# Moving the high part of the MLP input's last kt by 224 bytes, and its low part's product ahead of it

## The chip, the cores and the metric

The kernel runs on one core of a Trainium2 chip. The metric is the device time of one execution in microseconds (us). Three runs of the kernel before took 2049.33, 2052.9 and 2054.07 us; the median is 2052.9. One execution was also profiled, and each statement about single instructions comes from that trace. Engines are named as the profile names them: PE is TensorE's matmuls, PEld its weight loads, DVE is VectorE, ACT is ScalarE, POOL is GpSimd, SP is SyncE.

## The reference

A two-layer encoder trunk over 256 tokens of width 2048, in float32. Each layer has attention (neighbourhood attention in the first, grouped-query attention in the second, each beside four cross-attention heads into 256 memory tokens) and then a dense MLP. The part that the change touches is the MLP's first product:

```python
n = rms_norm(h, mlp_norm[i])
h = h + jnp.square(jax.nn.relu(n @ w_up[i])) @ w_down[i]
```

Here n is 256 x 2048, w_up 2048 x 8192 and w_down 8192 x 2048.

## The kernel before, in words

**Split operands.** Each float32 operand of a large product is held as two parts, high and low, both of the type fp32r: the high part is a rounded copy that ACT writes, the low part is the rest, which DVE computes. A product is then three matmuls that add into the same PSUM tile: high by high, high weights by low input, low weights by high input.

**The MLP's input.** `hT` is the normed input of the MLP, transposed, features on the 128 partitions: 16 kt of 128 features, and for each kt 512 elements along a partition, 256 tokens of the high part and then 256 of the low part. It lies in a tile of the tag "wide", made by `wide` (L434), which has 128 elements (512 bytes) of room beyond the 16 x 512 that it uses. `wide` takes an offset in bytes; `hT` uses 0, the attention input `nT` uses 480. `o_done` (L620) makes `hT` once in each layer (L628) and fills it kt by kt: `transposed` (L323) has PE transpose into PSUM, and `split_pair` (L335) has ACT write the high part and DVE the low part. After the last kt, DVE adds to `h` (L661).

**The up-projection.** A chunk of w_up is 128 columns wide, 64 chunks in each layer, 128 in all. For each chunk `u_products` (L707) runs over the 16 kt with three matmuls each, 48 in all, each with the weights stationary (128 x 128) and 256 tokens of `hT` moving: L713 is the high weights by the high input, L714 the high weights by the low input, L715 the low weights by the high input. The weights come as two halves of 8 kt, split by `half_of_side` (L717) into the tiles uh and ul.

**The down-projection and the order.** The 64 chunks are eight parts of eight. `add_mlp` (L948) plans part 0 of the up-projection alone, eight chunks in a row. From then on each chunk of part p + 1 goes together with one step of the down-projection of part p, 56 steps in each layer, 112 in all. Such a step is a sum of seven products in the manner of Strassen. `down_grains` (L785) makes it in two groups, FIRST with three products on the tiles bh and bl (nine matmuls), and SECOND with four on th and tl (twelve); here the activations a_s are stationary and 512 columns of weights move (L828 to L830). A scheduler orders the instructions of each engine; on PE it makes mostly the cycle: the 48 matmuls of a chunk, the 12 of SECOND, the 9 of FIRST, the next chunk. The weights' last part of eight goes through plain products (L217 to L221).

**Where tiles start.** Some tiles are placed at chosen offsets along the partition. `MOVING_AT` = 160 bytes is added to uh and ul where they are the moving operand of a plain product and not the stationary one of the up-projection.

The functions that the change touches, and what calls them:

Of the kernel before, what the change touches and what calls it, by code (L numbers as in the profile page):

```python
# [11 lines left out]
F32R = mybir.dt.float32r  # L12
# [5 lines left out]
P = 128  # L18
D = 2048
SEQ = 256  # L20
NT = SEQ // P
KT = D // P
# [18 lines left out]
GUARD = 3  # L41

MOVING_AT = 160
MASKED = -1e30


# [10 lines left out]
class Work:  # L57


    def __init__(self, kind, src, acts, first, begins, last, start, done):  # L60
        self.kind, self.src, self.acts = kind, src, acts
        self.first, self.begins, self.last, self.start, self.done = first, begins, last, start, done
        self.early = False


class Grain:
# [7 lines left out]
def encoder_kernel(ctx: ExitStack, tc: tile.TileContext, t: dict, out: bass.AP):  # L74
    nc = tc.nc
# [3 lines left out]
    def opened(name, side="left", space=None, bufs=1):  # L79
        kw = {"space": space} if space else {}  # L80
        manager = tc.tile_pool(name=name, bufs=bufs, side=side, reuse_waits="tile", **kw)
        pools[name] = manager, manager.__enter__()
        return pools[name][1]

    def closed(*names):
        for name in names:
            pools.pop(name)[0].__exit__(None, None, None)

    const = opened("const")
    keep = opened("keep")  # L90
# [28 lines left out]
    for j in range(8):  # L119
        s = slice(j * 512, (j + 1) * 512)  # L120
        nc.sync.dma_start(mem0[:, s], t["memT"][:, s])
        if j % 2 == 0:
            s = slice(j * 256, (j + 2) * 256)
# [25 lines left out]
    def halves_of(w):  # L149
# [6 lines left out]
        def prep_early(hf):  # L156
            tiles[hf] = half_of_side(tiles["raw"], hf, MOVING_AT)

# [39 lines left out]
    def later(n, fn, *args):  # L198
        pending.append((state["tick"] + n, fn, args))
# [124 lines left out]
    def transposed(dst, src, ks, which):  # L324

        for a in range(0, len(ks), 2):
            pt = at.att.tile([P, 2, SEQ], F32, tag="att", name="pt_n")
            for b, k in enumerate(ks[a : a + 2]):
                for i in range(NT):
                    nc.tensor.transpose(pt[:, b, i * P : (i + 1) * P], src(i, k), ident)  # L330
            for b, k in enumerate(ks[a : a + 2]):
                last = split_pair(dst, pt[:, b, :], which, k)
        return last
# [100 lines left out]
    def wide(name, at=0):  # L434
        room = keep.tile([P, KT * 512 + P], F32R, tag="wide", name=name)
        return room[:, at // 4 : at // 4 + KT * 512].rearrange("p (a b) -> p a b", b=512)

    def keys(name):
        return at.work.tile([P, NMH, 512], F32R, tag="keys", bufs=1, name=name)

# [160 lines left out]
    def sum_squares(which, i, nb):  # L601
        sq = at.side.tile([P, 512], BF16, tag="junk", bufs=1, name="sq")
        nc.scalar.activation(sq, h[:, i, nb * 512 : (nb + 1) * 512], AF.Square,
                             accum_out=ssq[which][:, i, nb : nb + 1])

    def mean_square(which, n, name):

        s = small.tile([P, NT], F32, tag="ss0", name="ss_t")
        nc.vector.tensor_reduce(s, ssq[which][:, :, :n], axis=AX.X, op=ALU.add)
        v = keep.tile([P, NT], F32, tag=name, name=name)  # L610
        nc.vector.tensor_scalar(v, s, 1.0 / (n * 512), EPS, op0=ALU.mult, op1=ALU.add)
        return v
# [7 lines left out]
    def o_done(layer, nb):  # L620
        which = 2 * layer

        def guard():

            box["near"] = mean_square(which, GUARD, "near")
            box["scale"] = keep.tile([P, NT], F32, tag="scale", name="scale")
            nc.gpsimd.tensor_tensor(box["scale"], box["near"], mhalf[:, :NT], op=ALU.pow)
            box["hT"] = wide(f"hT{layer}")  # L628

        def begun():  # L630

            y = at.side.tile([P, NT, 512], F32, tag="T", bufs=2, name="h_s")
            for i in range(NT):
                nc.scalar.activation(y[:, i, :], h[:, i, D - 512 :], AF.Copy, scale=box["scale"][:, i : i + 1])
            box["begun"] = y

        def scaled(b):
            y = at.side.tile([P, NT, 512], F32, tag="T", bufs=2, name="h_s")
            for i in range(NT):
                nc.scalar.activation(y[:, i, :], h[:, i, b * 512 : (b + 1) * 512], AF.Copy,  # L640
                                     scale=box["scale"][:, i : i + 1])
            transposed(box["hT"], lambda i, k: y[:, i, k % 4 * P : (k % 4 + 1) * P],
                       list(range(b * 4, b * 4 + 4)), (G_M0, G_M1)[layer])

        def inv():

            v = mean_square(which, 4, "full")
            box["inv"] = keep.tile([P, NT], F32, tag="inv", name="inv")
            nc.vector.reciprocal(v, v)
            nc.vector.tensor_tensor(box["inv"], v, box["near"], op=ALU.mult)  # L650
            box["ninv"] = keep.tile([P, NT], F32, tag="ninv", name="ninv")
            nc.vector.tensor_scalar(box["ninv"], box["inv"], -1.0, None, op0=ALU.mult)

        def f(w):
            if nb == 0:
                closed("work")
                at.side = opened("side", side="right")
            def add():
                for i in range(NT):
                    hs = h[:, i, nb * 512 : (nb + 1) * 512]  # L660
                    nc.vector.tensor_tensor(hs, w.ps[i], hs, op=ALU.add)  # L661

            def squares():
                for i in range(NT):
                    sum_squares(which, i, nb)

            if nb < 3:
                add()
                squares()
            if nb == GUARD - 1:  # L670
                later(1, guard)
                for b in range(GUARD):
                    later(2 + 2 * b, scaled, b)
                later(7, begun)
            if nb == 3:
                y = box["begun"]
                for i in range(NT):
                    nc.vector.scalar_tensor_tensor(y[:, i, :], w.ps[i], box["scale"][:, i : i + 1], y[:, i, :],
                                                   op0=ALU.mult, op1=ALU.add)
                box["ready"] = transposed(box["hT"], lambda i, k: y[:, i, k % 4 * P : (k % 4 + 1) * P],  # L680
                                          list(range(12, KT)), (G_M0, G_M1)[layer])
                later(8, past, add)
                later(10, past, squares)
                later(12, past, inv)
        return f
# [21 lines left out]
    def u_products(ps, k0, nk, hi, lo):  # L707

        acts = box["hT"]
        for j in range(nk):  # L710
            k = k0 + j
            s = slice(j * P, (j + 1) * P)
            nc.tensor.matmul(ps, hi[:, s], acts[:, k, :SEQ], start=k == 0, stop=False)  # L713
            nc.tensor.matmul(ps, hi[:, s], acts[:, k, SEQ:], start=False, stop=False)  # L714
            nc.tensor.matmul(ps, lo[:, s], acts[:, k, :SEQ], start=False, stop=k == KT - 1)  # L715

    def half_of_side(raw, hf, place=0):  # L717
        s = slice(place // 4, place // 4 + HALF)
        tiles = tuple(at.side.tile([P, HALF + 64], F32R, tag=n, bufs=2, name=n)[:, s] for n in ("uh", "ul"))
        box.setdefault("splits", []).append(split(*tiles, raw[:, hf * HALF : (hf + 1) * HALF]))  # L720
        return tiles
# [6 lines left out]
    def up_grains(layer, part, m):  # L728
# [8 lines left out]
        def run(hf):  # L737
            if hf == 0:
                if part == 0:
                    own["ps"] = at.acc.tile([P, 512], F32, tag="acc", name="ps_u")[:, :SEQ]  # L740
                else:
                    if part == 1 and m == 0:
                        closed("ps_att", "ps_acc")
                        at.sums = opened("ps_sums", space=bass.MemoryType.PSUM)
                        box["ps"] = {}
                        box["unused"] = set()
                    own["ps"] = at.sums.tile([P, 512], F32, tag="up", name="ps_u")[:, :SEQ]
            u_products(own["ps"], hf * (KT // 2), KT // 2, *own.pop(hf))
# [144 lines left out]
    def plain_grains(layer, nb):  # L893
# [9 lines left out]
        def prep(c, hf):  # L903
            if c == 0:
                own[c, hf] = half_of_side(own[0], hf, MOVING_AT)
            else:
# [275 lines left out]
def expanded_bias(rpb):  # L1182
# [6 lines left out]
    dc = np.clip(cols[None, :] - cols[:, None] + WIN_W - 1, 0, 2 * WIN_W - 2)  # L1189
    res = np.full((nh, 2, GRID_W, BJ, GRID_W), MASKED, np.float32)  # L1190
    for r in range(2):
        for j in range(BJ):
            dr = j + ROWS + 1 - r
            res[:, r, :, j, :] = np.where(inside[None], rpb[:, dr][:, dc], np.float32(MASKED))
    return res.reshape(nh, P, BJ * GRID_W)
# [64 lines left out]
```

## Time and profile before

| What | Value |
|---|---|
| Median of three runs | 2052.9 us |
| Profiled execution | 2051.05 us |
| Its span, first to last instruction | 2049.3 us |
| PE busy | 2029.9 us (99%) |
| Mean granted TensorE clock | 0.999 |
| Up-projection matmuls (L713, L714, L715) | 3 x 2048, of 128 x 256 |
| Down-projection matmuls on th and tl | 3 x 448, of 128 x 512 |
| Down-projection matmuls on bh and bl | 3 x 336, of 128 x 512 |

A row of a group in the profile gives the line, the engine, the operation, the tiles (written <- read), the shape, the count, then the busy time in us and the mean duration of one in ns, and last the idle time of the engine just before them with what ended it. Matmuls are pipelined: the next starts before the last has ended, and the ends are modelled. So the time from one start to the next says how fast PE goes, and the durations of one shape differ by as much as these steps do. A row of the timeline gives the start and the duration in us, the engine, the line, the operation and the tiles.

### The profile page before, as it was taken

How to read it: one execution, taken by the hardware profiler on the slowest of the kernel's cores; microseconds unless marked ns; L12 is line 12 of the kernel's file. 1: busy time of each engine (PE TensorE's matmuls, PEld its weight loads, DVE VectorE, ACT ScalarE, POOL GpSimd, SP SyncE). 2: the span in 40 equal slices, each digit the busy share in tenths (PEclk: the TensorE clock that was granted, in tenths of full speed). 3: DMA queues.
4: the chain of work that ended last, by engine and by line, in shares of the span. 5: the costliest groups of instructions: out<-in, count | busy, mean ns of one | idle time of the engine just before them, and what ended most of it. 6: DMA issues, size and time to landing. Idle time of an engine off the chain costs nothing.

```text
span 2049.3 us, 31582 instructions
## 1 busy us (share of the span) xinstructions
PE 2029.9 (99%) x12516; PEld 1813.1 (88%) x12516; DVE 1669.0 (81%) x2061; ACT 1252.6 (61%) x1652; POOL 119.3 (6%) x144
## 2 busy tenths in 40 slices
PE   8999999999999999999999999999999999999998
PEld 7888888889999999999988888889999999999996
DVE  6767666558999999999897667657989999999896
ACT  6755555556666666666656557556666666666664
POOL 0000000000000000000000001000000000000000
PEclk9999999999999999999999999999999999999999
DMA  7755554727777787787765554537877777777773
GB/s 280 283 190 179 190 176 169 276 86 228 230 231 231 218 242 226 222 245 220 231 219 200 180 184 144 187 122 222 246 228 228 224 230 228 231 230 226 232 222 132
DMA packets 93429, 433.79 MB, mean 212 GB/s; under 512 B 10464, under 2 KB 12128, under 8 KB 60128
## 3 DMA queue, kind: packets, MB, share of 16 engines
q1 hardware_dynamic: 75456, 398.47, 57.7%
q0 software_dynamic: 16816, 31.46, 8.7%
q8 instruction: 98, 1.61, 0.3%
q10 hardware_dynamic: 1008, 1.84, 0.3%
q14 instruction: 51, 0.42, 0.1%
HBM read 398.17 MB, written 4.19 MB: 196 GB/s over the span
## 4 chain that ended last, share of the span: by engine, by line
PE 98%; DVE 0%; ACT 0%; issue 0%; DMA 0%; POOLq 0%; POOL 0%; SPq 0%; ACTq 0%
PE ps_u L715 11%; PE ps_u L713 11%; PE ps_u L714 11%; PE p L828 9%; PE p L829 9%; PE p L830 9%; PE ps_m L217 8%; PE ps_m L220 8%; PE ps_m L221 8%; PE ps_s L230 7%; PE ps_s L233 3%; PE pt_a L393 1%; PE pt_n L330 1%; PE av L401 0%; PE sc_ps L367 0%
## 5 line engine op out<-in xcount | busy, mean ns | idle before, releaser
L715 PE MATMUL ps_u<-hT,ul 128*128 128x256 f32 x2048 | 568.4, 278 | 1.8 <-DVE ul L313 1.8
L713 PE MATMUL ps_u<-hT,uh 128*128 128x256 f32 x2048 | 568.6, 278 | 0.1
L714 PE MATMUL ps_u<-hT,uh 128*128 128x256 f32 x2048 | 568.0, 277 | 0.0
L312 ACT ACTIVATE uh<-raw_U 128x1024 fp32r<-128x1024 f32 x278 | 294.9, 1062 | 320.0 <-PE ps_u L714 302.1
L313 DVE TENSOR_TENSOR lo<-raw,hi 128x1024 fp32r<-128x1024 f32 (+1 forms) x220 | 261.4, 1194 | 164.6 <-ACT hi L312 162.1
L713 PEld LDWEIGHTS ps_u<-hT,uh 128*128 128x128 f32 x2048 | 384.9, 188 | 5.7 <-ACT uh L312 0.5
L715 PEld LDWEIGHTS ps_u<-hT,ul 128*128 128x128 f32 x2048 | 386.0, 189 | 3.6 <-DVE ul L313 2.6
L714 PEld LDWEIGHTS ps_u<-hT,uh 128*128 128x128 f32 x2048 | 384.4, 188 | 4.6
L313 DVE TENSOR_TENSOR ul<-raw_U,uh 128x1024 fp32r<-128x1024 f32 x278 | 337.6, 1219 | 40.0 <-ACT uh L312 39.8
L312 ACT ACTIVATE hi<-raw 128x1024 fp32r<-128x1024 f32 (+1 forms) x220 | 227.5, 1039 | 210.2 <-PE ps_m L221 119.0
L313 DVE TENSOR_TENSOR tl<-t,th 128x2048 fp32r<-128x2048 f32 x112 | 256.3, 2288 | 42.0 <-ACT th L312 41.8
L312 ACT ACTIVATE th<-t 128x2048 fp32r<-128x2048 f32 x112 | 215.1, 1921 | 123.2 <-PE p L830 118.6
L313 DVE TENSOR_TENSOR bl<-b,bh 128x1536 fp32r<-128x1536 f32 x112 | 196.1, 1751 | 0.3 <-ACT bh L312 0.2
L829 PE MATMUL p<-tl,a_s 128*128 128x512 f32 x448 | 177.2, 395 | 0.0
L830 PE MATMUL p<-th,a_s 128*128 128x512 f32 x448 | 174.4, 389 | 0.0
L312 ACT ACTIVATE bh<-b 128x1536 fp32r<-128x1536 f32 x112 | 166.2, 1484 | 7.4 <-PE p L830 1.3
L828 PE MATMUL p<-th,a_s 128*128 128x512 f32 x448 | 166.1, 395 | 0.0
L808 POOL DMA_DIRECT2D t<-b x112 | 97.1, 867 | 1160.8 <-ACT c L769 406.5
L230 PE MATMUL ps_s<-nT,hi 128*128 128x512 f32 x448 | 142.5, 397 | 0.0
L830 PE MATMUL p<-bh,a_s 128*128 128x512 f32 x336 | 131.1, 390 | 0.0
L829 PE MATMUL p<-bl,a_s 128*128 128x512 f32 x336 | 130.9, 390 | 0.0
L807 DVE TENSOR_TENSOR t<-t,b 128x512 f32<-128x512 f32 x112 | 77.1, 689 | 39.9 <-DMA t<-in_w_pair 35.0
(239 smaller groups left out, 3519.2 us busy)
## 6 DMA issues: line engine op xcount, KB each, us to landing
raw_U<-in_w_up SPq DMA_DIRECT2D x128, 1024.0 KB, 6.5
b<-in_w_pair SPq DMA_DIRECT2D x112, 768.0 KB, 4.6
raw<-in_w_o SPq DMA_DIRECT2D x32, 1024.0 KB, 4.9
t<-in_w_pair SPq DMA_DIRECT2D x112, 256.0 KB, 3.4
t<-b POOLq DMA_DIRECT2D x112, 256.0 KB, 6.8
raw<-in_w_b SPq DMA_DIRECT2D x21, 1024.0 KB, 5.0
raw<-in_w_av SPq DMA_DIRECT2D x12, 1024.0 KB, 4.9
raw<-in_w_aq SPq DMA_DIRECT2D x12, 1024.0 KB, 4.9
```

What stands on the lines that cost most here:

```text
L217: first = nc.tensor.matmul(w.ps[i], ah, hi[:, s], start=st, stop=False)
L220: nc.tensor.matmul(w.ps[i], ah, lo[:, s], start=False, stop=False)
L221: nc.tensor.matmul(w.ps[i], al, hi[:, s], start=False, stop=sp)
L230: nc.tensor.matmul(ps, hi[:, s], acts[:, k0 + j, :], start=k0 + j == 0, stop=False)
L312: first = nc.scalar.activation(dst_hi, src, AF.Copy)
L313: return first, nc.vector.tensor_tensor(dst_lo, src, dst_hi.bitcast(F32), op=ALU.subtract)
L713: nc.tensor.matmul(ps, hi[:, s], acts[:, k, :SEQ], start=k == 0, stop=False)
L714: nc.tensor.matmul(ps, hi[:, s], acts[:, k, SEQ:], start=False, stop=False)
L715: nc.tensor.matmul(ps, lo[:, s], acts[:, k, :SEQ], start=False, stop=k == KT - 1)
L828: nc.tensor.matmul(ps, a[:, 0, ai, :], hi[:, s], start=begins, stop=False)
L829: nc.tensor.matmul(ps, a[:, 0, ai, :], lo[:, s], start=False, stop=False)
L830: nc.tensor.matmul(ps, a[:, 1, ai, :], hi[:, s], start=False, stop=ends)
```

## The change

`hT` is now addressed through a small class. For the first 15 kt it gives the addresses of before. For the last kt the low part stands where the high one stood, and the high part 256 elements and 224 bytes (`LAST_AT`) further, in the room that the tile had beyond its 16 x 512 elements. In `u_products`, the last kt multiplies the high weights by the low part first and by the high part second. The third product is the same as before. The number and the shapes of all instructions stay.

```diff
+LAST_AT = 224
...
+class Shifted:
+    def __init__(self, room):
+        self.room = room
+
+    def __getitem__(self, key):
+        _, k, s = key
+        at = k * 512 + (s.start or 0)
+        if k == KT - 1:
+            at = k * 512 + (0 if s.start else SEQ + LAST_AT // 4)
+        return self.room[:, at : at + SEQ]
...
+    def shifted(name):
+        return Shifted(keep.tile([P, KT * 512 + P], F32R, tag="wide", name=name))
...
-            box["hT"] = wide(f"hT{layer}")
+            box["hT"] = shifted(f"hT{layer}")
...
-            nc.tensor.matmul(ps, hi[:, s], acts[:, k, :SEQ], start=k == 0, stop=False)
-            nc.tensor.matmul(ps, hi[:, s], acts[:, k, SEQ:], start=False, stop=False)
+            parts = (slice(0, SEQ), slice(SEQ, 512))
+            for n, x in enumerate(parts if k < KT - 1 else parts[::-1]):
+                nc.tensor.matmul(ps, hi[:, s], acts[:, k, x], start=k == n == 0, stop=False)
             nc.tensor.matmul(ps, lo[:, s], acts[:, k, :SEQ], start=False, stop=k == KT - 1)
```

## The prediction

> **What bounds the kernel now.** I read the page's first lines, then the chain of work that ended last, then the groups of the lines that the change touches and of the lines that follow them.
>
> ```profile
> span 2049.3 us, 31582 instructions
> PE 2029.9 (99%) x12516; PEld 1813.1 (88%) x12516; DVE 1669.0 (81%) x2061; ACT 1252.6 (61%) x1652; POOL 119.3 (6%) x144
> PE 98%; DVE 0%; ACT 0%; issue 0%; DMA 0%; POOLq 0%; POOL 0%; SPq 0%; ACTq 0%
> L715 PE MATMUL ps_u<-hT,ul 128*128 128x256 f32 x2048 | 568.4, 278 | 1.8 <-DVE ul L313 1.8
> L713 PE MATMUL ps_u<-hT,uh 128*128 128x256 f32 x2048 | 568.6, 278 | 0.1
> L714 PE MATMUL ps_u<-hT,uh 128*128 128x256 f32 x2048 | 568.0, 277 | 0.0
> L829 PE MATMUL p<-tl,a_s 128*128 128x512 f32 x448 | 177.2, 395 | 0.0
> L830 PE MATMUL p<-th,a_s 128*128 128x512 f32 x448 | 174.4, 389 | 0.0
> L828 PE MATMUL p<-th,a_s 128*128 128x512 f32 x448 | 166.1, 395 | 0.0
> L829 PE MATMUL p<-bl,a_s 128*128 128x512 f32 x336 | 130.9, 390 | 0.0
> ```
>
> TensorE carries 98% of the chain, and the idle time before the three up-projection lines is 1.9 us in all. No other engine can give time back, so the change counts only as far as matmuls start closer together or further apart. The numbers of matmuls stay: each of the 128 chunks of w_up takes 48 (16 kt of three). What can move is the step from one start to the next.
>
> The mean duration shows that step, because starts overlap: a duration is about 163 ns above the step to the next start. So I go by differences of durations within one width, and by starts in the timeline. One regular cycle of the MLP (a chunk of w_up, the 12 matmuls of SECOND on th and tl, the 9 of FIRST on bh and bl) looks like this, by groups in four windows: the first five matmuls of a chunk with the one before them, the middle of that chunk, its end with SECOND and FIRST, and a chunk of layer 0's part 0, where chunk follows on chunk.
>
> ```profile
> L713 PE MATMUL ps_u<-hT,uh 128*128 128x256 f32 x2 | 0.6, 284 | 0.0
> L714 PE MATMUL ps_u<-hT,uh 128*128 128x256 f32 x2 | 0.6, 282 | 0.0
> ...
> L713 PE MATMUL ps_u<-hT,uh 128*128 128x256 f32 x13 | 3.6, 276 | 0.0
> ...
> L829 PE MATMUL p<-tl,a_s 128*128 128x512 f32 x4 | 1.6, 397 | 0.0
> L828 PE MATMUL p<-th,a_s 128*128 128x512 f32 x4 | 1.6, 396 | 0.0
> L830 PE MATMUL p<-th,a_s 128*128 128x512 f32 x4 | 1.6, 389 | 0.0
> ...
> L829 PE MATMUL p<-bl,a_s 128*128 128x512 f32 x3 | 1.2, 389 | 0.0
> L715 PE MATMUL ps_u<-hT,ul 128*128 128x256 f32 x1 | 0.3, 280 | 0.0
> ...
> L714 PE MATMUL ps_u<-hT,uh 128*128 128x256 f32 x17 | 4.8, 281 | 0.0
> ```
>
> So one and the same matmul of 256 columns takes 276 ns at its best and 280 to 284 in three places: at the start of a chunk, as its last one, and all through some chunks. One of 512 columns takes 389 at its best and 396 or 397 just behind a chunk. The starts at one end of a chunk say the same:
>
> ```profile
> 548.51 0.28 PE L715 MATMUL ps_u<-hT,ul 128*128 128x256 f32 x1
> 548.63 0.40 PE L828 MATMUL p<-th,a_s 128*128 128x512 f32 x1
> ...
> 551.18 0.39 PE L830 MATMUL p<-th,a_s 128*128 128x512 f32 x1
> 551.41 0.39 PE L828 MATMUL p<-bh,a_s 128*128 128x512 f32 x1
> ...
> 553.45 0.28 PE L713 MATMUL ps_u<-hT,uh 128*128 128x256 f32 x1
> ```
>
> The nine of FIRST take 2.04 us, 227 ns each. The twelve of SECOND take 2.78 us where twelve times 227 is 2.72: **about 60 ns are lost behind each chunk**, and 4 more in its last matmul. Nothing waits there, the idle column is 0.0; these are slow steps. What changes at these places is the start address of the moving operand. In the built program hT's parts start 160 bytes past a multiple of 256, all 32 alike; th, tl, bh and bl start 128 past one. The stationary operands change too: uh and ul at 224 past, the activations a at 128. Inside a chunk nothing changes, and there the step is short.
>
> **The change part by part.** Order and waits first. On every engine the instructions are the same, in the same order; only the two matmuls of uh in the last kt change places, 128 times. ACT and DVE write the two parts of that kt in the order of before, so the first matmul on it in each layer now waits for DVE's part and not for ACT's. I cost that at nothing: DVE, in order, goes on to the add of L661 at 449.06 us, and the first matmul of the last kt is the fourth below, 1.85 us later. Had the cover gone, the price were one step, about 0.11 us, twice.
>
> ```profile
> 449.06 1.28 DVE L661 TENSOR_TENSOR h<-ps_m,h 128x512 f32<-128x512 f32 x2
> ...
> 450.91 0.28 PE L713 MATMUL ps_u<-hT,uh 128*128 128x256 f32 x1
> ```
>
> Addresses next. The low part now starts where the high one was, 160 past; the high part starts 1024 + 224 bytes further, which is 128 past a multiple of 256, as th does. The last three matmuls of a chunk read at 160, 128, 128, and the hand-over to th is at equal phase. The jump sits two matmuls earlier.
>
> What can be saved: the 60 ns behind a chunk and the 4 of its last matmul. Over the run, against 389 ns, the rows of th and tl give 448 x 6 + 448 x 6 + 448 x 0 ns = 5.4 us; 112 last matmuls by 4 ns are 0.4 us more. 5.8 us is the ceiling.
>
> What of it stays is not shown by any row directly, so I bound it by other places where matmuls of 256 columns hand over to matmuls of 512 whose moving operand starts at 128. Three such places, eleven steps each:
>
> ```profile
> 277.93 0.39 PE L220 MATMUL ps_m<-lo,nT 128*128 128x512 f32 x1
> ...
> 280.46 0.39 PE L217 MATMUL ps_m<-hi,nT 128*128 128x512 f32 x1
> ```
> ```profile
> 384.38 0.39 PE L220 MATMUL ps_m<-lo,cat 128*128 128x512 f32 x1
> ...
> 386.87 0.39 PE L217 MATMUL ps_m<-hi,cat 128*128 128x512 f32 x1
> ```
> ```profile
> 273.52 0.40 PE L217 MATMUL ps_m<-hi,nT 128*128 128x512 f32 x1
> ...
> 276.04 0.39 PE L221 MATMUL ps_m<-hi,nT 128*128 128x512 f32 x1
> ```
>
> Eleven steps at 226.7 ns are 2.49 us; these take 2.53, 2.49 and 2.52, so 37, 0 and 27 ns are lost. Behind a chunk of w_up the same count (548.63 to 551.18) is 2.55, which is 57. Undisturbed chunks thus give the worst entry I find. The first two places come from attention matmuls that start at 224, the third from matmuls that start at 128. I take the mean of the three, 21 ns, and keep 0 and 60 as ends.
>
> What is added: the last three matmuls of a chunk now stand at the jump. By the rows of a chunk's start a matmul near a jump takes 6 to 8 ns more than 276; I take 6 for each of three, 18, of which 4 were paid before: 14 more (ends: 8 and 20).
>
> The sum: 60 - 21 - 14 = 25 ns for each regular chunk. In 14 of the 112 chunks, seven in each layer, FIRST falls in after the chunk's second matmul, as here:
>
> ```profile
> 706.71 0.28 PE L714 MATMUL ps_u<-hT,uh 128*128 128x256 f32 x1
> 706.83 0.39 PE L829 MATMUL p<-bl,a_s 128*128 128x512 f32 x1
> ...
> 713.63 0.39 PE L828 MATMUL p<-th,a_s 128*128 128x512 f32 x1
> ...
> 716.38 0.62 PE L828 MATMUL p<-bh,a_s 128*128 128x512 f32 x2
> ```
>
> There the twelve of SECOND take 2.75 us and lose some 27 ns already, no more than I expect to stay; I count the other 98. 98 x 25 ns = 2.45 us less. Part 0 has chunk upon chunk, 14 boundaries in two layers, where the new phase jumps back to 160. Those of layer 0 run at 281 already (the L714 row of 17 above), those of layer 1 at 276 (the row below), across their boundaries too. Seven boundaries then pay the start of a chunk, about 33 ns (five steps, 6 to 8 each), and the 14: 7 x 47 ns = 0.3 us more.
>
> ```profile
> L714 PE MATMUL ps_u<-hT,uh 128*128 128x256 f32 x17 | 4.7, 276 | 0.0
> ```
>
> That makes 2.1 us less: 2051.05 us for the profiled execution (1.75 above its span) becomes 2048.9. The median of the three runs, 2052.9, lies 1.85 above that execution, so the forecast is **2050.8 us**.
>
> A rule of the Trainium skill speaks against all of this. SBUF — State Buffer, Who interferes with whom, gives TensorE two read ports of its own and says that it never waits for anyone; TensorE: Matmul & The Clock Gate, Part 2, adds that loading the next weights takes no read bandwidth from the running matmul. By that no start address would matter, and the time would stay at 2052.9. The trace disagrees as far as steps of equal matmuls go (276 against 284 ns); it does not show what collides.
>
> **The rivals.**
>
> Clean hand-over: equal phase is all that SECOND needs, as at 384.38 us, and nothing is lost behind a chunk. Three matmuls at 5 more (the 281 of the slow chunk) less the 4 of before cost 11: 98 x (60 - 11) = 4.8 us, 0.3 back in part 0, so 4.5 us less, 2048.4 us. For it: of the entries quoted, the one behind a chunk is the worst, and only there does the phase jump by 32 bytes. Against it: the third place above came at equal phase and lost 27.
>
> Width, not address: the loss comes with the change from 256 to 512 columns and back, for both always fall together here. Then the move of an address does nothing: 2052.9 us. Against it: at 384.38 us the same change of width lost nothing. This is also the case in which the change doesn't do what it says.
>
> Slower: the change of the stationary operand's phase, 224 to 128, is what sets SECOND off, and it stays, so the 60 ns stay. The new jump then only adds: three matmuls at 8 more, less 4, are 20 ns on 112 chunks, 2.2 us. In part 0 the jump back tips the seven quick chunks into the slow pace: 7 x 48 x 5 ns = 1.7 us, and 14 jumps by 47 ns are 0.7 us. 4.6 us more: 2057.5 us. It decides from about 56 ns lost behind a chunk upwards; below that the saving covers the jumps. For it: both phases change at that place, and the rows can't part them.
>
> **How the numbers follow.** A measurement of this kernel can tell about 0.2%, 4.1 us, from no change. The forecast gets 0.42, the clean hand-over 0.33, width 0.10, slower 0.15. Faster by over 0.2%: the clean hand-over and a twentieth from the forecast's better end, 0.38. Slower: 0.15. Within: 0.47. The range reaches from the clean hand-over less half of the runs' own spread (2049.33 to 2054.07, so 2.4 us), 2046.0, to just short of the slower rival's price, 2056.5.
>
> **What would show it.** In the profile of the changed kernel SECOND's rows for th and tl at 389 to 391 mean a clean hand-over, at 392 to 393 the forecast, at 395 or more that the stationary operand or the width decides. The last three matmuls of a chunk should stand at 280 to 284. Part 0's chunks at 281 in layer 1 would show the tip into the slow pace. The forecast is wrong if the middle of regular chunks leaves 276, or if a wait appears before the first matmul of the last kt.

## The result, and the profile after

The changed kernel took **2048.26 us** (median of 20 runs, 2046.84 to 2052.62). In the same series the kernel before took 2051.17 us (median of 20, 2049.07 to 2057.59). The ratio is 0.9985, with a 95% interval of 0.9979 to 0.9991: about 2.9 us less, between 1.8 and 4.3. Before's median had been 2052.9 us over the three runs that the forecast started from, so 1.7 us of the distance between the forecast and the result are the spread of before.

The page of the kernel after: the span, the engines, the chain of work by engine, and the groups of the up-projection (the two products with uh have one line now, L735), of SECOND (L849 to L851 on th and tl) and of FIRST (here bl).

```profile
span 2046.4 us, 31582 instructions
...
PE 2026.7 (99%) x12516; PEld 1813.8 (89%) x12516; DVE 1667.0 (81%) x2061; ACT 1251.6 (61%) x1652; POOL 119.2 (6%) x144
...
PE 93%; DVE 3%; DMA 2%; issue 1%; ACT 0%; POOLq 0%; POOL 0%; SPq 0%; DVEq 0%; ACTq 0%
...
L735 PE MATMUL ps_u<-hT,uh 128*128 128x256 f32 x4096 | 713.2, 278 | 0.2
...
L736 PE MATMUL ps_u<-hT,ul 128*128 128x256 f32 x2048 | 568.9, 278 | 1.6 <-DVE ul L330 1.5
...
L850 PE MATMUL p<-tl,a_s 128*128 128x512 f32 x448 | 174.8, 390 | 0.0
L851 PE MATMUL p<-th,a_s 128*128 128x512 f32 x448 | 174.3, 389 | 0.0
...
L849 PE MATMUL p<-th,a_s 128*128 128x512 f32 x448 | 164.1, 391 | 0.0
...
L850 PE MATMUL p<-bl,a_s 128*128 128x512 f32 x336 | 131.0, 390 | 0.0
```

The two slow groups of SECOND fell from 395 ns to 390 and 391. FIRST and the up-projection keep their means. One regular cycle by groups, in a window over SECOND and FIRST, and the starts at the end of its chunk (first column: start in us):

```profile
L849 PE MATMUL p<-th,a_s 128*128 128x512 f32 x4 | 1.6, 390 | 0.0
L850 PE MATMUL p<-tl,a_s 128*128 128x512 f32 x4 | 1.6, 390 | 0.0
L851 PE MATMUL p<-th,a_s 128*128 128x512 f32 x4 | 1.6, 389 | 0.0
```

```profile
548.11 0.40 PE L735 MATMUL ps_u<-hT,uh 128*128 128x256 f32 x2
548.34 0.28 PE L736 MATMUL ps_u<-hT,ul 128*128 128x256 f32 x1
548.46 0.40 PE L849 MATMUL p<-th,a_s 128*128 128x512 f32 x1
...
551.19 0.39 PE L849 MATMUL p<-bh,a_s 128*128 128x512 f32 x1
```

SECOND takes 551.19 - 548.46 = 2.73 us for its twelve matmuls, where it took 2.78. The last three matmuls of the chunk (a row with x2 stands for two in a row) take 0.35 us, 0.01 more than three steps at their best.

To see where the rest went, I took every start of the MLPs in the trace and counted each step above the quickest one of its width (113.3 ns for 256 columns, 226.7 ns for 512) as lost. First the losses in ns of a regular cycle (medians of 96), then all losses in us, each step in one row only:

| What | before | after |
|---|---|---|
| first six matmuls of a chunk, ns | 33 | 32 |
| the 39 in the middle, ns | 0 | 0 |
| last three, ns | 4 | 9 |
| SECOND, twelve, ns | 62 | 10 |
| FIRST, nine, ns | 1 | 2 |
| the 96 regular cycles, us | 9.55 | 5.18 |
| the 16 other cycles, 14 of them split, us | 3.48 | 3.54 |
| the 16 chunks of part 0, us | 5.89 | 6.76 |
| all other steps, us | 1.91 | 2.43 |

So 4.4 us came out of the regular cycles; 0.9 went back in part 0 and 0.5 in other steps. That leaves 2.9, which is what the spans differ by (2049.3 and 2046.4). Part 0 of layer 1, by groups in a window over one of its chunks:

```profile
L735 PE MATMUL ps_u<-hT,uh 128*128 128x256 f32 x24 | 4.3, 281 | 0.0
L736 PE MATMUL ps_u<-hT,ul 128*128 128x256 f32 x13 | 3.7, 281 | 0.0
```

It stood at 276 before. Five of its chunks went from no loss to 214 or 220 ns each (32 at the start, 173 in the middle, 15 at the end); the last chunk gives back some of it, since its step at a wait for ul costs 0.12 us where it cost 0.47. The other steps hold three new waits, 0.25, 0.22 and 0.11 us, all in cycles where the order is not the regular one; the step behind two of them is slow by 0.11 us more, which the table has in the row of the 16 other cycles. Here is the first, in the chain of waits in order of time (start, length, what it was) and in the timeline of PE:

```profile
773.82 3.75 DMA t<-in_w_pair
...
788.65 1.15 DVE ul L330
789.84 0.39 PE ps_u L736
```

```profile
789.36 0.40 PE L851 MATMUL p<-bh,a_s 128*128 128x512 f32 x1
789.84 0.39 PE L736 MATMUL ps_u<-hT,ul 128*128 128x256 f32 x1
```

The step from 789.36 to 789.84 is 0.48 us where it should be 0.23. The up-projection waits for DVE's ul, and behind that, sixteen microseconds back, for DVE's wait for a DMA of the weights t. That is why PE's share of the chain falls from 98% to 93%; the length of such a piece is not lost time, only what PE waits at its end. That a quicker SECOND brings this path up to PE is not shown: a second profile of the same kernel (the last experiment) has none of these waits, and a kernel whose SECOND is as slow as before's (256, below) waits for DVE's tl by 1.3 us.

### The profile page after: what moved, and what is told of

Same layout as the page of the kernel before. It is cut to its first block, busy times and chain, and to the rows that moved or that the text cites. A ratio compares the mean times of both kernels' runs of the same rounds, so it can differ in the third digit from the quotient of the medians.

```text
span 2046.4 us, 31582 instructions
## 1 busy us (share of the span) xinstructions
PE 2026.7 (99%) x12516; PEld 1813.8 (89%) x12516; DVE 1667.0 (81%) x2061; ACT 1251.6 (61%) x1652; POOL 119.2 (6%) x144
## 4 chain that ended last, share of the span: by engine, by line
PE 93%; DVE 3%; DMA 2%; issue 1%; ACT 0%; POOLq 0%; POOL 0%; SPq 0%; DVEq 0%; ACTq 0%
PE ps_u L735 21%; PE ps_u L736 11%; PE ps_m L234 8%; PE ps_m L237 8%; PE ps_m L238 8%; PE p L849 8%; PE p L850 8%; PE p L851 8%; PE ps_s L247 7%; PE ps_s L250 3%; DMA t<-in_w_pair 1%; DVE tl L330 1%; PE pt_a L410 1%; DVE ul L330 1%; PE pt_n L347 1%
## 5 line engine op out<-in xcount | busy, mean ns | idle before, releaser
L735 PE MATMUL ps_u<-hT,uh 128*128 128x256 f32 x4096 | 713.2, 278 | 0.2
L735 PEld LDWEIGHTS ps_u<-hT,uh 128*128 128x128 f32 x4096 | 627.4, 188 | 10.3 <-ACT uh L329 0.6
L851 PE MATMUL p<-th,a_s 128*128 128x512 f32 x448 | 174.3, 389 | 0.0
L849 PE MATMUL p<-th,a_s 128*128 128x512 f32 x448 | 164.1, 391 | 0.0
L851 PE MATMUL p<-bh,a_s 128*128 128x512 f32 x336 | 131.1, 390 | 0.0
L849 PE MATMUL p<-bh,a_s 128*128 128x512 f32 x336 | 108.0, 389 | 0.0
L237 PE MATMUL ps_m<-lo,nT 128*128 128x512 f32 x264 | 103.7, 393 | 0.0
```

Source lines behind the costliest of these rows:

```text
L237: nc.tensor.matmul(w.ps[i], ah, lo[:, s], start=False, stop=False)
L735: nc.tensor.matmul(ps, hi[:, s], acts[:, k, x], start=k == n == 0, stop=False)
L849: nc.tensor.matmul(ps, a[:, 0, ai, :], hi[:, s], start=begins, stop=False)
L851: nc.tensor.matmul(ps, a[:, 1, ai, :], hi[:, s], start=False, stop=ends)
```

## The experiments

All times are medians; the kernel before ran in the same series each time. The theory was: the phase of the moving operand's start (its address modulo 256 bytes) at the hand-over from a chunk to SECOND sets what SECOND loses, and neither the order of the two products nor the stationary operand does. Numbers such as 32/0/9/10 are the losses in ns of a regular cycle's first six matmuls, middle, last three and SECOND, as in the table above.

**One half of the change alone.** Order only:

```diff
-        if k == KT - 1:
-            at = k * 512 + (0 if s.start else SEQ + LAST_AT // 4)
```

> The low part's product comes first in the last kt, but the high part stays where it was, 160 bytes past a multiple of 256. Phase theory (what counts is the start address modulo 256 bytes at the hand-over to th): no address changes its phase, so SECOND on th loses 57 to 62 ns behind each chunk as before, L715's last matmul stays at 280 ns, and the time is that of before (within 0.1%, about 2051 us). Order theory (which product comes last but one is what helps): SECOND loses about 10 ns as in the changed kernel, and the time is 0.15% lower.

2050.64 us against 2050.97, ratio 1.0 (0.9991 to 1.001). The rows of SECOND in its profile, grouped over the whole run:

```profile
L847 PE MATMUL p<-tl,a_s 128*128 128x512 f32 x448 | 177.2, 396 | 0.0
...
L846 PE MATMUL p<-th,a_s 128*128 128x512 f32 x448 | 166.1, 395 | 0.0
```

These are before's rows, and the cycle loses 32/0/4/62. The order by itself does nothing in a regular cycle. Part 0 is another matter: layer 0's chunks, at 281 in the profile of before, stand at 276 in this one, with every start at 160 in both:

```profile
L732 PE MATMUL ps_u<-hT,uh 128*128 128x256 f32 x26 | 4.5, 276 | 0.0
```

So where no jump stands between the chunks of part 0, their pace differs from one profile to the next, and the 0.9 us that part 0 costs in the change is counted from one such profile.

Place only:

```diff
-            for n, x in enumerate(parts if k < KT - 1 else parts[::-1]):
+            for n, x in enumerate(parts):
```

> The high part of the last kt lies where the changed kernel has it, but its product comes first as before, so the starts go 160, 128, 160, 128 through the last kt and into th. Phase theory: the hand-over to th is at equal phase as in the changed kernel, but three jumps lie in the last kt in place of one; the last matmuls cost 280 to 284 ns each, and what SECOND loses is that of the entry's state, between 10 and 40 ns. I expect about 25 ns, and a time between the two kernels, 0.05% to 0.15% below before. Order theory: no gain at all without the order, SECOND loses 57 to 62 ns.

2046.35 us against 2050.97, ratio 0.9981 (0.9971 to 0.999). SECOND over the whole run, and part 0 of layer 1 in a window:

```profile
L850 PE MATMUL p<-tl,a_s 128*128 128x512 f32 x448 | 174.8, 390 | 0.5 <-DVE tl L330 0.5
...
L849 PE MATMUL p<-th,a_s 128*128 128x512 f32 x448 | 164.0, 391 | 0.0
```

```profile
L735 PE MATMUL ps_u<-hT,uh 128*128 128x256 f32 x22 | 3.9, 277 | 0.0
L736 PE MATMUL ps_u<-hT,ul 128*128 128x256 f32 x11 | 3.0, 277 | 0.0
```

The whole gain in SECOND comes with the address alone (33/0/9/10), with the stationary operands and the widths where they were. That decides against the width and against the stationary operand. The 25 ns that were expected did not come: three jumps in the last kt cost SECOND no more than one. And part 0 of layer 1 runs at 277, where the change has 281 (layer 0 likewise): with the address moved, the slow pace comes with the new order. That rests on one profile of this kernel and on three with the order (224 twice, 480 below). Between this kernel and the change the intervals of the times overlap; that the order costs about a microsecond is read from the steps, not from the times.

**Is it the phase, and is 256 its period?** The same kernel with `LAST_AT` at 256 (the high part starts 160 past a multiple of 256 again) and at 480 (128 past one, as with 224):

> As the changed kernel, but the high part lies 256 bytes further on and not 224: it moves as far, but keeps the phase of 160. Phase theory: SECOND loses 57 to 62 ns, as before; part 0 of layer 1 stays at 276 ns; time as before, 2051 us. Theory that the distance between low and high part (more than the 1024 bytes of before) is what helps: SECOND loses about 10 ns, time as the changed kernel.

> As the changed kernel, but 480 bytes further on, which is 224 plus 256: the start differs modulo 512 and is equal modulo 256. Phase theory with a period of 256 bytes: same as the changed kernel, SECOND loses about 10 ns behind a regular chunk, the last three matmuls 0, 5 and 5 ns, part 0 of layer 1 at 281 ns, time within 0.05% of it. If the period is 512 or the distance counts, SECOND loses something else, 25 to 62 ns.

At 256: 2050.84 us against 2050.97, ratio 0.9997 (0.9988 to 1.0007). At 480: 2048.8 against 2050.97, ratio 0.999 (0.9981 to 1.0). SECOND on tl, grouped over the whole run, at 256 and then at 480:

```profile
L850 PE MATMUL p<-tl,a_s 128*128 128x512 f32 x448 | 177.5, 396 | 1.4 <-DVE tl L330 1.3
```

```profile
L850 PE MATMUL p<-tl,a_s 128*128 128x512 f32 x448 | 175.1, 391 | 0.0
```

A shift by 256 bytes leaves before's 62 ns behind a chunk, and one by 480 gives the 10 ns of 224. So it is not the distance that acts, and not the free room, but the phase. A period of 128 is not excluded: no two of the phases tried are 128 apart. At 480 part 0 of layer 1 is slow too:

```profile
L735 PE MATMUL ps_u<-hT,uh 128*128 128x256 f32 x21 | 3.8, 281 | 0.0
```

**Other phases for the last high part.** `LAST_AT` at 192 and at 32 puts it at 96 and at 192 past a multiple of 256, so that a jump of 32 or 64 bytes stays at the hand-over, and one more stands two matmuls earlier. One run each:

> As the changed kernel, but 192 bytes further on: the last kt's high part starts 96 past a multiple of 256, 32 short of th's 128. Equal-phase theory: the hand-over to th jumps by 32 again, SECOND loses about 60 ns. State theory (SECOND loses its 62 ns only if the jump is met at the quick pace; any jump two matmuls earlier takes the chunk off that pace): it loses less, 10 to 40 ns, though the phases differ.

> As the changed kernel, but 32 bytes further on: the high part starts 192 past a multiple of 256, and the hand-over to th is a jump of 64 down. Equal-phase theory: SECOND loses 60 ns or more. State theory: 10 to 40 ns, as the other shifts that take the chunk off the quick pace.

2047.28 and 2046.93 us, beside 2050.58 of before. The first start of SECOND and the first of FIRST, at 192 and then at 32:

```profile
547.00 0.39 PE L849 MATMUL p<-th,a_s 128*128 128x512 f32 x1
...
549.74 0.39 PE L849 MATMUL p<-bh,a_s 128*128 128x512 f32 x1
```

```profile
546.79 0.39 PE L849 MATMUL p<-th,a_s 128*128 128x512 f32 x1
...
549.54 0.39 PE L849 MATMUL p<-bh,a_s 128*128 128x512 f32 x1
```

SECOND takes 2.74 and 2.75 us and loses 24 and 30 ns (33/0/15/24 and 32/0/9/30). So equal phase leaves least, but it is not needed for half of the gain: 62 ns came only where a chunk at the quick pace kept its phase up to the jump. Part 0 is quick here, but for one chunk of layer 1 behind a wait at 192, although the low part comes first as in the change:

```profile
L735 PE MATMUL ps_u<-hT,uh 128*128 128x256 f32 x22 | 3.8, 278 | 0.0
```

```profile
L735 PE MATMUL ps_u<-hT,uh 128*128 128x256 f32 x22 | 3.9, 276 | 0.0
```

So the order does not tip part 0 by itself either; the row of phases at a boundary does (160, 128, 128, then 160 again in the change; 128, 160, 128 with place only; 160, 96, 96 and 160, 192, 192 here).

**One phase for the whole chunk.** If equality at the hand-over were all, one could place the whole of hT, or uh and ul, so that one of the operands never jumps. First the stationary uh and ul at the activations' phase, 128 in place of 224, then hT at 128 in place of 160, each made from the kernel before:

```diff
-            own[hf] = half_of_side(own["raw"], hf)
+            own[hf] = half_of_side(own["raw"], hf, MOVING_AT)
```

```diff
-            box["hT"] = wide(f"hT{layer}")
+            box["hT"] = wide(f"hT{layer}", 224)
```

> The kernel before, with the up-projection's weights (stationary) moved from 224 to 128 bytes past a multiple of 256, which is the phase of the activations that are stationary in SECOND. The moving input stays at 160. Theory that the moving operand's phase sets SECOND off: it still loses about 60 ns behind a regular chunk. Rival, that the stationary operand's phase does: the loss falls to 0 to 10 ns. Either way the pace inside a chunk may leave 276 ns, since the distance of the two phases changes; if it goes to 281 everywhere, 6144 matmuls by 5 ns are about 30 us more.

> The kernel before, with the whole MLP input at 128 and no jump of the moving operand anywhere; the stationary operand still changes from 224 to 128 and back. Moving-phase theory: SECOND loses 0 to 25 ns behind a chunk and the first five matmuls of a chunk lose less than 33 ns together, 4 to 8 us less in all, if the pace inside a chunk stays at 276 ns. Stationary theory: both losses stay, 60 and 33 ns. If the pace inside a chunk depends on the distance of moving and stationary phase, it goes to about 281 ns and the kernel loses up to 30 us: that would say why only the last kt can be moved.

2060.05 us against 2051.17, ratio 1.0041 (1.0027 to 1.0055), and 2064.21, ratio 1.006 (1.0045 to 1.0075). The up-projection and SECOND on tl in each, grouped over the whole run:

```profile
L713 PE MATMUL ps_u<-hT,uh 128*128 128x256 f32 x2048 | 571.4, 279 | 0.0
...
L829 PE MATMUL p<-tl,a_s 128*128 128x512 f32 x448 | 175.4, 392 | 0.0
```

```profile
L713 PE MATMUL ps_u<-hT,uh 128*128 128x256 f32 x2048 | 573.3, 280 | 0.0
...
L829 PE MATMUL p<-tl,a_s 128*128 128x512 f32 x448 | 175.4, 391 | 0.0
```

Cycles lose 22/130/10/24 and 25/155/13/32. SECOND gains 38 and 30 ns, but every matmul in the middle of a chunk loses 3.3 to 4 ns, 39 times. 96 cycles by 87 and by 127 ns are 8.4 and 12.2 us, nearly all of the 8.9 and 13.0 us measured. Inside a chunk 160 for the moving and 224 for the stationary operand, at its quick pace, is the good pair of the three tried, and only a chunk's ends may leave it.

What SECOND lost here, 24 and 32 ns, neither theory had expected. With all of hT at 128 the moving operand does not jump, and 32 ns are lost all the same: equal phase alone is not a clean hand-over. With the weights at 128 the stationary operand does not jump, and the loss falls from 62 to 24. But both kernels run their chunks off the quick pace, and before's split chunks, off it too, also lose 24, with both jumps in place. So these two runs do not part the stationary operand's phase from the pace.

**The chunk's start too.** hT moves up by 256 bytes, and the high part of the first kt starts 128 past a multiple of 256, as bl before it. In one kernel its two products come first (128, 128, 160), in the other the order of before stays (128, 160, 128). The last kt has the change's address and the order of before in both.

```diff
-        at = k * 512 + (s.start or 0)
+        at = k * 512 + 64 + (s.start or 0)
+        if k == 0:
+            at = SEQ + 64 if s.start else LAST_AT // 4
...
+            three = [(hi, high), (hi, low), (lo, high)]
+            if k == 0:
+                three = [(hi, high), (lo, high), (hi, low)]
```

> As the address-only kernel (the last kt's high part at 128, its product first), and the first kt's high part at 128 too, with the order high by high, low weights by high, high weights by low, so that FIRST hands over to the chunk at equal phase and the jump comes two matmuls later. State theory (a loss depends on the pace at which the jump is met, and a jump met off the quick pace costs less): the start of a chunk loses 10 to 25 ns in place of 33, the end stays at 9 + 10 ns, 1 to 2 us less than the address-only kernel (2046 us), so about 2045 us. Rival (each jump costs its own amount wherever it is): 33 ns or more stay, time as the address-only kernel or up to 1 us more.

> As the kernel with both high parts at 128, but the first kt in the order of before, so that the starts of a chunk go 128, 160, 128, 160: three jumps at the start of a chunk, as the address-only kernel has three at its end. State theory: the alternation costs no more than one jump at the end did (9 + 10 ns), so 10 to 25 ns in place of 33 at the start. Rival: three jumps cost more than one, over 33 ns, and the kernel is slower than the address-only one by up to 2 us.

2046.46 us against 2051.17, ratio 0.9974 (0.9962 to 0.9986), and 2047.7, ratio 0.9987 (0.9978 to 0.9996). At the start of a regular chunk the two products first save 8 ns (25 in place of 33, the weak end of what was expected), and the order of before saves none, where 8 to 23 were expected. The larger effect stands elsewhere. The split chunks, into which FIRST falls after the second matmul, ran at 281 before; here are the rows for one of them, of the kernel after and then of the kernel with the two products first, each in a window behind the split:

```profile
L735 PE MATMUL ps_u<-hT,uh 128*128 128x256 f32 x26 | 4.6, 281 | 0.0
L736 PE MATMUL ps_u<-hT,ul 128*128 128x256 f32 x12 | 3.4, 281 | 0.0
```

```profile
L741 PE MATMUL ps_u<-hT,uh 128*128 128x256 f32 x26 | 4.5, 276 | 0.0
L741 PE MATMUL ps_u<-hT,ul 128*128 128x256 f32 x13 | 3.6, 276 | 0.0
```

39 matmuls at 4.5 ns less are about 0.17 us in each. In the other kernel the split chunks stay slow but for one, and part 0 alternates, about 223 ns lost in one chunk and 43 in the next. In the one with the two products first part 0 is slow in both layers (281), with 226 ns lost in each chunk, which takes back part of it:

```profile
L741 PE MATMUL ps_u<-hT,uh 128*128 128x256 f32 x22 | 3.9, 281 | 0.0
```

**The pieces put together.** The kernel with the two products first, and in the first seven chunks of part 0 the low part of the last kt first. The change ran again in the same series.

```diff
+            if k == KT - 1 and box["row"]:
+                three = [(hi, low), (hi, high), (lo, high)]
...
+            box["row"] = part == 0 and m < PK - 1
```

> As the kernel with the mirrored first kt, except that in part 0 (chunk upon chunk, all but its last) the last kt's low part comes first, so that both jumps between chunks go away: 160, 128, 128, then 128, 128, 160. If jumps between chunks tip part 0 into the slow pace, its chunks go to 276 ns and 14 x 0.17 = 2.4 us are saved, about 2044 us. If the two jumps inside the chunk's ends do it, part 0 stays at 281 and the time at 2046.5 us.

> The changed kernel once more, beside the others on the same chip. It should give 0.9985 of before again (0.9979 to 0.9991), SECOND 10 ns, and layer 1's part 0 at 281 ns; if part 0 in layer 1 shows 276 ns this time, the slow pace there is chance and not the work of the order.

2043.54 us (2043.0 to 2044.36) against 2050.58 of before, ratio 0.9969 (0.9957 to 0.9981), the fastest of all; the change 2047.22 (2046.57 to 2050.99), ratio 0.9988 (0.9979 to 0.9997). Their ranges do not meet. The span of the first, and its part 0 of layer 1 in a window:

```profile
span 2041.2 us, 31582 instructions
```

```profile
L741 PE MATMUL ps_u<-hT,uh 128*128 128x256 f32 x22 | 3.8, 278 | 0.0
```

Against the second profile of the change its losses fall by 0.6 us in the regular cycles, by 2.3 us in the 16 others of the 112 chunks and by 0.9 us in part 0. That is 3.8 us in all. The medians differ by 3.7; the two profiled spans differ by 4.8, because the first chunk of layer 0 also starts 1.0 us sooner (441.3 and 442.3 us). And the rows of the change's second profile, over the whole run and in part 0, stand where those of its first did:

```profile
L850 PE MATMUL p<-tl,a_s 128*128 128x512 f32 x448 | 174.7, 390 | 0.0
```

```profile
L735 PE MATMUL ps_u<-hT,uh 128*128 128x256 f32 x21 | 3.8, 281 | 0.0
```

## Why the prediction was right, and where it was off

- **What bounds the kernel.** Right: PE's steps moved the time, at the places named (SECOND, the chunk's end, part 0). Order only leaves the time where it was; the cover for the wait before the last kt held.
- **Which of the two phases.** For the 62 ns the moving operand's, as the forecast had it. Place only shows it against the width and against the stationary operand, and 256 and 480 show that it is the phase and not the distance. That the stationary phase counts for nothing is not shown (24 ns with the weights at 128). The forecast read the Trainium skill (SBUF — State Buffer, Who interferes with whom), where TensorE never waits for anyone, as a rule by which no start address would matter; for this step that does not hold: one start address, moved alone, gives 0.9981 (0.9971 to 0.999).
- **What stays behind a chunk.** The forecast took 21 ns of 60, the mean of three entries elsewhere; 10 stay. The entries were no measure for this one: how much SECOND loses depends on the phases of the last matmuls before it, as 24 and 30 ns at other phases show. By the forecast's own sign (SECOND's rows at 389 to 391) this is the clean hand-over, its first rival, and not the forecast's partial one.
- **What is added at the chunk's end.** The term of 14 ns was mis-sized: 5 more than before, not 14. The first of the three loses nothing, the other two 5 ns each.
- **The sum per cycle.** 25 ns forecast, 45 measured (the mean of 96 cycles; 98 were counted, but the first cycle of each layer behind part 0 is not regular either). This is the term that was too small, by 1.9 us over the run.
- **Split chunks.** No gain, as forecast (24 ns before, 25 after, where all of SECOND follows). This held for the change only: place only has 10 there.
- **Part 0.** Failed. The forecast kept layer 1's chunks in their quick pace and counted 0.3 us; it put the tip into the slow pace into the slower rival, at 1.7 us for seven chunks. The tip came without that rival's other half, and with it part 0 costs 0.9 us more than in the profile of before. It came with the address and the new order together (224 and 480), and not with the address alone; with the order alone the pace is not settled.
- **Waits.** Counted at nothing; 0.58 us in this profile (0.8 with the slow steps behind them), and none in the change's second profile, so this is no fixed cost.

The two misses had opposite signs, 1.9 us too little saved and 0.6 us too little paid back, with 0.58 us of waits; that -2.1 us forecast and -2.9 measured lie so close is in part luck. The clean hand-over's 49 ns per cycle were nearer to the 45 measured than the forecast's 25; its 4.5 us did not come, because part 0 and the other steps took back 1.4. The time alone would have hidden this.

What stays open: why these addresses are slow, why SECOND's first two steps still lose 5 and 4 ns and the other ten nothing, and by which rule a row of phases leads into the quick or the slow pace. The runs show that the row matters and that a wait can change the pace too, not how.

## What to carry to other kernels

Where PE is the bound and nothing waits, compare the steps of equal matmuls by place: here 4 to 5 ns in each of 896 make the gain, and no idle column shows them. Move one start address at a time, and look after each move at all places that read the operand, since the phase that is best at a hand-over was worse by 3 to 4 ns in each matmul inside the chunk. A change made of an address and an order should be run in halves: here the address brought all of the gain, and the order, by the steps, cost about a microsecond.

## What the runs showed of the hardware that I had not expected

- The step of these fp32r matmuls depends on where the operands start modulo 256 bytes: 113.3 ns at the quick pace for 256 columns with the moving operand at 160 and the stationary at 224, about 117 ns with 160 and 128 or with 128 and 224 (mean durations over the run 278, 279 and 280 ns). A shift of the last high part by 256 changes nothing (ratio 0.9997, 0.9988 to 1.0007).
- One and the same chunk at the same addresses has two paces, 276 and 281 ns, which is 173 ns over the 39 matmuls of its middle, and in these profiles keeps the one in which it starts until a jump or a wait. Where chunk follows chunk without a jump, the pace of before differs between its two layers (281 and 276), and with order only it changed once behind a wait. Where a jump stands at each boundary, the pace settles at one value within a chunk or two, in both layers, for the kernels with place only, at 224 and at 480; with jumps at both ends of a chunk and the order of before it alternates from chunk to chunk (223 and 43 ns lost).
